# Scores of two attention heads in one group of products, in turn on the upper and the lower 64 rows of the array

## The chip, the cores and the metric

The kernel runs on one core of a Trainium2 chip. The metric is the device time of one execution in microseconds (us). Each kernel is run several times on the same chip, and a profiled execution leaves the trace from which the rows below are taken. The engines are named as in the profile: PE is the matrix unit TensorE and PEld its weight loads, DVE the vector engine, ACT the scalar engine, POOL GpSimd, and SP the engine whose queue issues the DMA transfers.

## The reference

The program is two blocks of two layers each, on 256 rows of width 1024. The change lies in the second block. Each of its layers projects the normed rows by `w_in`, runs three attentions over the 256 positions, merges them by `w_out`, and adds a cross-attention to a memory of 256 rows. Two of the three attentions matter here, each with six heads of dimension 64:

```
def moba_attention(q, k, v):              # 6 heads; 256 positions are a single block of 256,
    ...                                   # so each query sees only its own block, causally
    s_own = jnp.einsum('bhqd,bhld->bhql', qi, ko).astype(jnp.float32) * scale
    s_own = jnp.where(to[None, :] <= tq[:, None], s_own, -jnp.inf)
    p = jax.nn.softmax(jnp.concatenate([s_sel, s_own], axis=-1), axis=-1)
    ...
def stick_breaking_attention(q, k, v):    # 6 heads, strictly causal
    ...
    z = jnp.einsum('bhqd,bhkd->bhqk', qi, k).astype(jnp.float32) * scale
    mask = kpos[None, :] < (q0 + jnp.arange(Q_BLOCK))[:, None]
    log_beta = jax.nn.log_sigmoid(z)
    log_1m_beta = jnp.where(mask, log_beta - z, 0.0)
    between = lax.cumsum(log_1m_beta, axis=3, reverse=True) - log_1m_beta
    w = jnp.where(mask, jnp.exp(log_beta + between), 0.0)
    ...
```

The third, `diff`, has eight score heads of dimension 32 and is not changed.

## The kernel before

Every product of fp32 data is made of three products of rounded halves: a value is stored as a high part and a low part (`HH` and `HL` for the normed rows, `wh` and `wl` for weights), and high×high, high×low and low×high are added up in PSUM. `linear` and `linear_T` do this for the projections, with all 128 rows of the array, in products of 512, 384 or 256 columns into the PSUM tiles `lin`. Their weights are split into halves on ACT, DVE and POOL as they arrive.

The queries and keys of `moba` and of `stick` lie transposed in the tiles `QA` and `KX` of shape [128, 2, 3, 256]: head h is on partitions 0 to 63 if h is even and on 64 to 127 if it is odd, the second index is the high or the low part, the third the pair of heads. A score product therefore contracts over 64 partitions and uses the upper or the lower 64 rows of the array. `head_terms` lists a head's three (query, key) terms. Each head needs six products: for `moba` three of 128 columns (queries 0 to 127 against keys 0 to 127) and three of 256 (queries 128 to 255 against all keys), followed in `causal_scores` by a product that adds the mask (`identb` as weights, `trib` streamed); for `stick` three of 256 columns and three of 128, with the keys as weights. That is 24 heads in the two layers and 144 such products. They are written to a PSUM bank of the ring `aux`, which has four banks and is shared with transposes and other small products.

What follows a `moba` head is `causal_P`: for each of its two query tiles a maximum on DVE (`tensor_reduce`), and an exponential on ACT that also adds up its row; then a reciprocal, a scaling, three transposes on PE, and the product with the values for two heads at once (`pair_out`). After a `stick` head come absolute value, exponential and logarithm on ACT, differences on DVE, a mask on POOL, a product with a triangle of ones (`sums`), an exponential, and `pair_out`. `pipeline` writes the stages of six heads in a staggered order.

The order in which instructions stand in each engine's queue is not that in which the code is written. Every call goes to an object of the class `Plan`, which records an operation with its predecessors and an assumed cost (`cost`), and at the end `order` lays all of them out with a list scheduler (`run_list`) and issues them. Some operations may go to one of two engines (`either`), and that too is decided there. An operation is one call, so the scheduler is free to put other products between two products of one head; only what is written under `joined()` becomes one operation, whose instructions stay together. All instructions have the line of the call in `issue` (L459 before), so rows are told apart by their tiles.

Of the kernel before, what the change touches and what calls it, by code (L numbers as in the profile page):

```python
# [182 lines left out]
class Plan:  # L183
# [24 lines left out]
        self.later = {}  # L208

    @contextmanager  # L210
    def joined(self):


        self.joint = []
        yield
        self.joint = None

    def where(self, v):
# [247 lines left out]
class Net:  # L466
# [1219 lines left out]
    def causal_P(self, ps, first=None):  # L1686
# [9 lines left out]
        nc.vector.reciprocal(ri, rs)  # L1696
        return P, ri

    def causal_scores(self, terms):

        nc = self.nc
        ps = self.aux_ps()
        for qt in range(2):
            o = ps[:, 0:128] if qt == 0 else ps[:, 128:384]
            for a, (q, k) in enumerate(terms):
                nc.tensor.matmul(o, q[:, qt * 128:qt * 128 + 128], k[:, :128 * (qt + 1)],
                                 start=qt == 0 and a == 0, stop=False, skip_group_check=True)
        nc.tensor.matmul(ps.rearrange("p (a b) -> p a b", a=2)[:, :, 0:128], self.identb,
                         self.trib.unsqueeze(1).to_broadcast([128, 2, 128]), start=False, stop=True, skip_group_check=True)
        return ps  # L1710

    def causal_T(self, P):
# [48 lines left out]
    def moba(self, z, v, g, mh, ml):  # L1761
        nc = self.nc
        q = self.t([128, 2, 3, 256], F32R, "QA")
        k = self.t([128, 2, 3, 256], F32R, "KX")
        for t in range(2):
            self.partial_rope(z[:, t].rearrange("p (h d) -> p h d", h=12), self.cs16, t, 12, 16)
            for a, dst, scale in ((0, q, 0.125), (1, k, 1.0)):
                ps = self.aux_ps()
                for c in range(3):
                    nc.tensor.transpose(ps[:, c * 128:c * 128 + 128], z[:, t, (3 * a + c) * 128:(3 * a + c + 1) * 128], self.ident)  # L1770
                s = slice(t * 128, t * 128 + 128)
                self.split_evac(dst[:, 0, :, s], dst[:, 1, :, s], ps[:, :384].rearrange("p (c q) -> p c q", c=3), scale)
        self.silu_T(g)
        st = {}

        def scores(h):
            P, ri = self.causal_P(self.causal_scores(self.head_terms(q, k, h)))
            for qt, sl in ((0, slice(0, 128)), (1, slice(128, 384))):
                self.scaled(P[:, sl], P[:, sl], ri[:, qt:qt + 1])
            st[h] = P  # L1780

        def transposes(h):
            st[h] = self.causal_T(st[h])

        def values(h):
            if h % 2:
                self.pair_out(h // 2, [st.pop(h - 1), st.pop(h)], v, g[:, h // 2], mh[:, h // 2], ml[:, h // 2])
        self.pipeline(((scores, 0), (transposes, 2), (values, 3)), 6, 1300)
# [87 lines left out]
    def stick(self, q, k, v, g, mh, ml):  # L1876
        nc = self.nc
        self.silu_T(g)
        diag = (slice(0, 128), slice(256, 384))
        st = {}  # L1880

        def scores(h):
            ps = self.aux_ps()
            terms = self.head_terms(q, k, h)
            for o, ks, qs in ((ps[:, 0:256], slice(0, 128), slice(0, 256)), (ps[:, 256:384], slice(128, 256), slice(128, 256))):
                for a, (qq, kk) in enumerate(terms):
                    nc.tensor.matmul(o, kk[:, ks], qq[:, qs], start=a == 0, stop=a == 2, skip_group_check=True)
            zz = ps[:, 0:384]
            e = self.t([128, 384], F32, "S2")
            nc.scalar.activation(e, zz, AF.Abs)  # L1890
            nc.scalar.activation(e, e, AF.Exp, scale=-1.0)
            nc.scalar.activation(e, e, AF.Ln, bias=1.0, scale=1.0)
            lb = self.t([128, 384], F32, "PT")
            nc.vector.scalar_tensor_tensor(out=lb, in0=zz, scalar=0.0, in1=e, op0=ALU.min, op1=ALU.subtract)
            nc.vector.tensor_tensor(out=e, in0=lb, in1=zz, op=ALU.subtract)
            for d in diag:
                nc.gpsimd.tensor_tensor(out=e[:, d], in0=e[:, d], in1=self.strict, op=ALU.mult)
            st[h] = lb, e

        def sums(h):  # L1900
            lb, e = st[h]
            pb = self.aux_ps()
            nc.tensor.matmul(pb[:, 0:256], self.suf, e[:, 0:256], start=True, stop=False, skip_group_check=True)
            nc.tensor.matmul(pb[:, 128:256], self.ones, e[:, 256:384], start=False, stop=True, skip_group_check=True)
            nc.tensor.matmul(pb[:, 256:384], self.suf, e[:, 256:384], start=True, stop=True, skip_group_check=True)
            nc.vector.tensor_tensor(out=lb, in0=pb[:, 0:384], in1=lb, op=ALU.add)
            nc.scalar.activation(lb, lb, AF.Exp)
            for d in diag:
                nc.gpsimd.tensor_tensor(out=lb[:, d], in0=lb[:, d], in1=self.strict, op=ALU.mult)

        def values(h):
            if h % 2:
                self.pair_out(h // 2, [st.pop(h - 1)[0], st.pop(h)[0]], v, g[:, h // 2], mh[:, 5 + h // 2], ml[:, 5 + h // 2])
        self.pipeline(((values, 2), (sums, 1), (scores, 0)), 6, 2600)

    def keep_clock(self, n, a, b):
# [130 lines left out]
```

## Time and profile before

| | before |
|---|---|
| median of 3 runs | 2108.07 us (2106.64 to 2111.05) |
| the profiled execution's own time | 2108.64 us |
| its span in the trace | 2106.9 us |
| PE busy | 1871.4 us (89%) |
| DVE, ACT, POOL busy | 894.2, 851.7, 299.0 us |
| mean granted clock of PE | 0.936 |

The span runs from the first to the last instruction of the trace; the time of the execution is 1.7 us longer. A busy share is an average over stages with different limits. The second block begins at about 1703 us; in each of its layers `stick` comes first, then `diff`, then `moba`.

### The profile page before, as it was taken

The page shows a single profiled execution, that of the slowest core. Times are in us where ns is not written, and L with a number is a line of the kernel's source. Part 1 is how long each engine was busy: PE and PEld are TensorE (multiplying, and loading weights), DVE is VectorE, ACT ScalarE, POOL GpSimd, SP SyncE. Part 2 cuts the span into 40 slices and gives each one's busy share as a digit, 9 for nine tenths or more (in the row PEclk, how much of TensorE's full clock was granted, in tenths as well). Part 3 has the DMA queues.
Part 4 walks back from the last instruction along what each step waited for, and adds up shares of the span by engine and source line. Part 5 has one row for each costly group of instructions (what it writes and reads, how often), then busy time and mean ns, then how long its engine had stood idle before and what let it go on. Part 6 is the DMA issues. An engine that isn't in the chain of part 4 may idle for free.

```text
span 2106.9 us, 29479 instructions
## 1 busy us (share of the span) xinstructions
PE 1871.4 (89%) x11564; PEld 1155.5 (55%) x11564; DVE 894.2 (42%) x1871; ACT 851.7 (40%) x1874; POOL 299.0 (14%) x383
## 2 busy tenths in 40 slices
PE   7999999999999898879999996757666799999998
PEld 4666767774443232226666762323222287889787
DVE  3855786681020201007855720101010176766766
ACT  3664666562222122016754531101010166676666
POOL 1302330230000000004401300000000023222321
PEclk9999999999999999999999997777767699999999
DMA  9667563678999999996667799999999963345332
GB/s 336 233 227 270 183 240 123 220 269 326 400 401 421 422 421 421 422 413 222 221 220 261 280 354 419 421 421 421 420 421 421 378 189 91 116 140 170 91 121 70
DMA packets 150347, 611.72 MB, mean 290 GB/s; under 512 B 10144, under 2 KB 32320, under 8 KB 96192
## 3 DMA queue, kind: packets, MB, share of 16 engines
q1 hardware_dynamic: 150208, 609.84, 75.7%
q8 instruction: 91, 1.49, 0.3%
q14 instruction: 48, 0.39, 0.1%
HBM read 606.63 MB, written 3.16 MB: 289 GB/s over the span
## 4 chain that ended last, share of the span: by engine, by line
PE 61%; DMA 26%; DVE 6%; POOL 3%; ACT 2%; issue 2%; SPq 0%; POOLq 0%; DVEq 0%; ACTq 0%
PE lin L459 45%; PE aux L459 14%; DMA W<-w_up_e 5%; DMA W<-w_gate_e 3%; PE acc L459 2%; DMA M<-w_up_e 2%; DMA Z<-w_gate_e 2%; DMA Z<-w_down_e 2%; DMA G<-w_up_e 2%; DMA G<-w_gate_e 2%; DVE S L459 1%; POOL sm L459 1%; DVE wl L459 1%; ACT S L459 1%; DMA DFT<-w_down_e 1%
## 5 line engine op out<-in xcount | busy, mean ns | idle before, releaser
L459 DVE TENSOR_TENSOR wl<-W,wh 128x512 fp32r<-128x512 f32 (+1 forms) x509 | 355.4, 702 | 184.2 <-ACT wh L459 180.8
L459 ACT ACTIVATE wh<-W 128x512 fp32r<-128x512 f32 (+1 forms) x449 | 271.9, 608 | 284.9 <-PE lin L459 216.2
L459 DVE TENSOR_TENSOR S<-lin,S 128x512 f32<-128x512 f32 (+1 forms) x32 | 17.8, 558 | 601.1 <-PE lin L459 601.1
L459 POOL TENSOR_TENSOR wl<-W,wh 128x512 fp32r<-128x512 f32 (+1 forms) x67 | 87.9, 1315 | 923.6 <-DMA W<-w_in 419.5
L459 ACT ACTIVATE S<-lin 32x512 f32<-32x512 f32 (+2 forms) x94 | 52.1, 555 | 398.7 <-PE lin L459 397.9
L459 PE MATMUL lin<-wl,HH 128*128 128x512 f32 (+1 forms) x600 | 208.3, 400 | 3.7 <-DVE wl L459 3.0
L459 PE MATMUL lin<-wh,HL 128*128 128x512 f32 (+1 forms) x600 | 204.9, 394 | 2.8 <-DVE HL L459 1.7
L459 PE MATMUL lin<-wh,HH 128*128 128x512 f32 (+1 forms) x600 | 206.1, 398 | 0.0
L459 PE MATMUL lin<-W,S 128*32 128x256 f32 (+1 forms) x960 | 109.5, 520 | 44.1 <-DMA W<-w_gate_e 14.9
L459 PE MATMUL aux<-cst,S 128*128 128x128 f32 x620 | 124.2, 290 | 27.4 <-DVE S L459 20.2
L459 PEld LDWEIGHTS aux<-cst,S 128*128 128x128 f32 x620 | 82.2, 153 | 88.7 <-DVE S L459 41.2
L459 PEld LDWEIGHTS lin<-wl,HH 128*128 128x128 f32 x600 | 107.7, 190 | 34.4 <-DVE wl L459 9.5
L459 PEld LDWEIGHTS lin<-wh,HL 128*128 128x128 f32 x600 | 108.8, 189 | 26.4 <-issue 6.7
L459 PEld LDWEIGHTS lin<-wh,HH 128*128 128x128 f32 x600 | 108.4, 189 | 26.6 <-issue 5.6
L459 ACT ACTIVATE S<-aux 128x512 f32<-128x512 f32 (+4 forms) x134 | 64.9, 489 | 125.0 <-PE aux L459 124.2
L459 PE MATMUL lin<-wh,OL 128*128 128x512 f32 x272 | 95.3, 402 | 1.5 <-DVE OL L459 1.5
L459 PEld LDWEIGHTS lin<-W,S 128*32 128x32 f32 (+1 forms) x960 | 36.7, 135 | 104.4 <-issue 32.9
L459 ACT ACTIVATE S<-aux,sm 128x256 f32<-128x256 f32 (+2 forms) x136 | 71.4, 527 | 31.6 <-DVE sm L459 29.1
L459 PE MATMUL lin<-Z,S 128*32 128x256 f32 (+1 forms) x528 | 67.2, 522 | 17.4 <-DMA Z<-w_up_e 9.0
L459 POOL TENSOR_SCALAR sm<-sm 128x1 f32<-128x1 f32 (+3 forms) x42 | 17.2, 409 | 439.3 <-ACT G L459 383.5
L459 DVE TENSOR_REDUCE sm<-aux 128x1 f32<-128x512 f32 (+3 forms) x136 | 66.1, 500 | 26.8 <-PE aux L459 25.6
L459 PE MATMUL lin<-wh,OH 128*128 128x512 f32 x208 | 75.8, 404 | 1.5 <-ACT wh L459 1.1
(412 smaller groups left out, 3393.1 us busy)
## 6 DMA issues: line engine op xcount, KB each, us to landing
W<-w_up_e SPq DMA_DIRECT2D x65, 1024.0 KB, 18.8
W<-w_in SPq DMA_DIRECT2D x62, 1024.0 KB, 5.4
W<-w_ada SPq DMA_DIRECT2D x40, 1024.0 KB, 5.0
G<-w_gate_e SPq DMA_DIRECT2D x36, 1024.0 KB, 17.4
W<-w_down_e SPq DMA_DIRECT2D x33, 1024.0 KB, 18.5
Z<-w_gate_e SPq DMA_DIRECT2D x24, 1024.0 KB, 18.0
W<-w_in SPq DMA_DIRECT2D x32, 768.0 KB, 4.7
DFT<-w_gate_e SPq DMA_DIRECT2D x23, 1024.0 KB, 19.8
```

The lines of the kernel that those rows point to most:

```text
L459: fn(*(self.real(a) for a in args), **{k: self.real(a) for k, a in kw.items()})
```

## The change

`pair_scores` forms the scores of two heads (2c and 2c+1) as one joined operation of twelve products. Its loops run over the two column ranges, within these over the three terms, and innermost over the two heads, so that successive products use the upper and the lower 64 rows in turn, and write two different banks of `aux`. The scheduler is told a cost for the whole (`joined(cost)`): 3 × (128+256) × 0.45 = 518 ns. The mask product is cut out of `causal_scores` into `causal_mask`, which `moba` calls for both heads after the pair's products. In `stick` the flag that starts a bank afresh stands only on a bank's first product, where before each of the two column ranges had its own. Nothing else differs, and `diff` calls `causal_scores` as before.

```diff
-    def joined(self):
+    def joined(self, cost=None):
         self.joint = []
         yield
+        if cost is not None:
+            self.alts[self.joint[0]] = {0: cost}
         self.joint = None
...
+    def causal_mask(self, ps):
+        self.nc.tensor.matmul(ps.rearrange("p (a b) -> p a b", a=2)[:, :, 0:128], self.identb,
+                              self.trib.unsqueeze(1).to_broadcast([128, 2, 128]), start=False, stop=True, skip_group_check=True)
+
+    def pair_scores(self, pair, out):
+        pss = [self.aux_ps() for _ in pair]
+        n = len(pair[0])
+        with self.nc.joined(sum(3 * (m.stop - m.start) * 0.45 for _, m, _ in out)):
+            for i, (o, m, st) in enumerate(out):
+                for a in range(n):
+                    for ps, terms in zip(pss, pair):
+                        mov, sta = terms[a]
+                        self.nc.tensor.matmul(ps[:, o], sta[:, st], mov[:, m], start=i == 0 and a == 0, stop=a == n - 1, skip_group_check=True)
+        return pss
+
     def causal_scores(self, terms):
...
-        nc.tensor.matmul(ps.rearrange("p (a b) -> p a b", a=2)[:, :, 0:128], self.identb,
-                         self.trib.unsqueeze(1).to_broadcast([128, 2, 128]), start=False, stop=True, skip_group_check=True)
+        self.causal_mask(ps)
         return ps
...
         def scores(h):
-            P, ri = self.causal_P(self.causal_scores(self.head_terms(q, k, h)))
+            if h % 2 == 0:
+                pair = [[(kk, qq) for qq, kk in self.head_terms(q, k, h + j)] for j in range(2)]
+                out = ((slice(0, 128), slice(0, 128), slice(0, 128)), (slice(128, 384), slice(0, 256), slice(128, 256)))
+                st["ps"] = self.pair_scores(pair, out)
+                for ps in st["ps"]:
+                    self.causal_mask(ps)
+            P, ri = self.causal_P(st["ps"][h % 2])
...
         def scores(h):
-            ps = self.aux_ps()
-            terms = self.head_terms(q, k, h)
-            for o, ks, qs in ((ps[:, 0:256], slice(0, 128), slice(0, 256)), (ps[:, 256:384], slice(128, 256), slice(128, 256))):
-                for a, (qq, kk) in enumerate(terms):
-                    nc.tensor.matmul(o, kk[:, ks], qq[:, qs], start=a == 0, stop=a == 2, skip_group_check=True)
-            zz = ps[:, 0:384]
+            if h % 2 == 0:
+                out = ((slice(0, 256), slice(0, 256), slice(0, 128)), (slice(256, 384), slice(128, 256), slice(128, 256)))
+                st["ps"] = self.pair_scores([self.head_terms(q, k, h + j) for j in range(2)], out)
+            zz = st["ps"][h % 2][:, 0:384]
```

The scheduler lays the second block out anew. On PE, DVE, ACT and POOL the order up to the second block is the same in both kernels, and the order of DMA transfers on SP is the same throughout. Three places on PE show what moves.

The first is PE near the start of the first `stick`, where before the first products of two heads stand: `aux_1` is the bank of one head, `aux_3` that of another, `lin` products of 384 columns around them.

```order
L459 MATMUL lin_0_217<-wh_2_205,HL_18_9773 128x384
L459 MATMUL lin_0_217<-wh_0_200,HH_19_9760 128x384
L459 MATMUL aux_1_340<-QA_6_9925,KX_7_10011 128x256
L459 MATMUL aux_3_122<-QA_6_9925,KX_7_10011 128x256
L459 MATMUL lin_2_277<-wl_0_212,HH_19_9760 128x384
L459 MATMUL lin_0_217<-wl_0_212,HH_19_9760 128x384
```

After the change the same `lin` products stand there without them.

```order
L461 MATMUL lin_0_217<-wh_2_205,HL_18_9773 128x384
L461 MATMUL lin_0_217<-wh_0_200,HH_19_9760 128x384
L461 MATMUL lin_2_277<-wl_0_212,HH_19_9760 128x384
L461 MATMUL lin_0_217<-wl_0_212,HH_19_9760 128x384
L461 MATMUL lin_2_277<-wh_0_200,HL_18_9773 128x384
```

The second place is a little later on PE, where the rest of the first head's scores stand before, each product alone or nearly so between `lin` products.

```order
L459 MATMUL lin_2_277<-HH_19_9760,wh_2_205 128x256
L459 MATMUL aux_1_340<-QA_6_9925,KX_7_10011 128x256
L459 MATMUL lin_2_277<-HH_19_9760,wl_2_215 128x256
L459 MATMUL aux_1_340<-QA_6_9925,KX_7_10011 128x128
L459 MATMUL lin_2_277<-HL_18_9773,wh_2_205 128x256
L459 MATMUL aux_1_340<-QA_6_9925,KX_7_10011 128x128
L459 MATMUL lin_0_217<-wh_0_200,HH_19_9760 128x512
L459 MATMUL aux_1_340<-QA_6_9925,KX_7_10011 128x128
L459 MATMUL lin_0_217<-wl_0_212,HH_19_9760 128x512
L459 MATMUL lin_0_217<-wh_0_200,HL_18_9773 128x512
```

After the change the whole group of the first two heads stands here, in the banks `aux_1` and `aux_2` in turn; six of its twelve products follow with 128 columns.

```order
L461 MATMUL lin_2_277<-HL_18_9773,wh_2_205 128x256
L461 MATMUL lin_0_217<-wh_0_200,HH_19_9760 128x512
L461 MATMUL aux_1_340<-QA_6_9925,KX_7_10016 128x256
L461 MATMUL aux_2_119<-QA_6_9925,KX_7_10016 128x256
L461 MATMUL aux_1_340<-QA_6_9925,KX_7_10016 128x256
L461 MATMUL aux_2_119<-QA_6_9925,KX_7_10016 128x256
L461 MATMUL aux_1_340<-QA_6_9925,KX_7_10016 128x256
L461 MATMUL aux_2_119<-QA_6_9925,KX_7_10016 128x256
```

What stood strewn over some 140 rows of PE (two heads) is one piece. The third place is PE in the first `moba`. Before, a head's products alternate with `lin` products of 256 columns (`acc` is a product of another attention).

```order
L459 MATMUL lin_1_220<-HH_19_9760,wh_2_205 128x256
L459 MATMUL aux_1_340<-KX_8_10868,QA_7_10882 128x128
L459 MATMUL lin_1_220<-HH_19_9760,wl_2_215 128x256
L459 MATMUL aux_1_340<-KX_8_10868,QA_7_10882 128x128
L459 MATMUL lin_1_220<-HL_18_9773,wh_2_205 128x256
L459 MATMUL aux_1_340<-KX_8_10868,QA_7_10882 128x256
L459 MATMUL lin_1_220<-HH_19_9760,wh_2_205 128x256
L459 MATMUL aux_1_340<-KX_8_10868,QA_7_10882 128x256
L459 MATMUL lin_2_277<-HH_19_9760,wh_2_205 128x256
```

After the change the heads stand in groups of twelve. Between the mask products of the second pair, in the banks `aux_3` and `aux_0`, and the group of the third pair, which has the same two banks, these rows are found (ahead of them come the second mask and four more `lin` products of 256 columns):

```order
L461 MATMUL lin_2_277<-HH_19_9760,wl_2_215 128x256
L461 MATMUL lin_2_277<-HL_18_9773,wh_2_205 128x256
L461 MATMUL lin_0_217<-wh_0_200,XC_3_10397 128x512
L461 MATMUL lin_1_220<-wh_0_200,XC_3_10397 128x512
L461 MATMUL lin_0_217<-wl_0_212,XC_3_10397 128x512
L461 MATMUL lin_1_220<-wl_0_212,XC_3_10397 128x512
L461 MATMUL lin_0_217<-wh_0_200,KC_18_10401 128x512
L461 MATMUL lin_1_220<-wh_0_200,KC_18_10401 128x512
L461 MATMUL aux_1_340<-cst,S_3_224 128x128 x3
L461 MATMUL aux_3_122<-KX_8_10916,QA_7_10906 128x128
L461 MATMUL aux_0_177<-KX_8_10916,QA_7_10906 128x128
```

Third and second pair are parted by six `lin` products of 256 columns, six of 512 and three transposes.

## Rows read from the trace of the kernel before

**Rows 1.** The page, busy time, share of the span and instructions of each engine.
```profile
PE 1871.4 (89%) x11564; PEld 1155.5 (55%) x11564; DVE 894.2 (42%) x1871; ACT 851.7 (40%) x1874; POOL 299.0 (14%) x383
```

**Rows 2.** Windows: stretch, us, busy PE, PEld, DVE, ACT, POOL; clock, DMA share, GB/s.
```profile
1733.00:1777.00 44.00, 44.00 (x207) 31.87 (x206) 28.51 (x57) 24.89 (x51) 16.00 (x27) 1.00 0.31 90
1777.00:1806.00 29.00, 28.17 (x184) 25.60 (x182) 25.32 (x72) 23.08 (x65) 12.75 (x19) 1.00 0.45 135
1806.00:1842.00 36.00, 35.95 (x224) 28.27 (x224) 23.00 (x61) 21.10 (x62) 3.60 (x6) 0.95 0.30 104
```

**Rows 3.** Waits in 1733 to 1842: waited for, us in total, times, longest.
```profile
ACT wh L459 <- PE lin L459: 18.3, 20, 3.4
...
PE aux L459 <- DVE S L459: 0.9, 1, 0.9
```

**Rows 4.** Windows of the tile QA alone: busy PE, PEld, DVE, ACT; clock, DMA, GB/s.
```profile
1703.00:1777.00 74.00, 9.63 (x36) 5.62 (x36) 1.09 (x3) 1.08 (x3) 1.00 0.45 135
...
1908.00:1981.00 73.00, 9.75 (x36) 5.73 (x36) 0.27 (x1) 0.00 (x0) 0.98 0.45 135
...
sum 218.00, PE 34.61 PEld 21.18 DVE 3.55 ACT 3.07; mean PE 8.65 PEld 5.29 DVE 0.89 ACT 0.77
```

**Rows 5.** Timeline of PE in `stick`: start, us, what; x2 is two in succession.
```profile
1733.67 0.61 PE L459 MATMUL lin<-wh,HH 128*128 128x512 f32 x2
1734.12 0.61 PE L459 MATMUL lin<-wl,HH 128*128 128x512 f32 x2
1734.67 0.50 PE L459 MATMUL aux<-QA,KX 64*128 64x256 f32 x2
...
1735.76 0.43 PE L459 MATMUL aux<-QA,KX 64*128 64x128 f32 x2
...
1736.79 0.33 PE L459 MATMUL aux<-QA,KX 64*128 64x128 f32 x1
...
1737.62 0.63 PE L459 MATMUL lin<-wh,HL 128*128 128x512 f32 x2
```

**Rows 6.** Timeline of PE in `moba`, single products, and two `lin` products in succession.
```profile
1815.56 0.32 PE L459 MATMUL aux<-KX,QA 64*128 64x128 f32 x1
...
1816.13 0.38 PE L459 MATMUL aux<-KX,QA 64*128 64x256 f32 x1
...
2029.34 0.28 PE L459 MATMUL lin<-HH,wl 128*128 128x256 f32 x1
2029.46 0.28 PE L459 MATMUL lin<-HL,wh 128*128 128x256 f32 x1
```

**Rows 7.** Timeline of PE in `moba`, strings of nine and of six on one half.
```profile
1822.56 1.29 PE L459 MATMUL aux<-KX,QA 64*128 64x128 f32 x9
...
1827.75 0.63 PE L459 MATMUL lin<-wl,XC 128*128 128x512 f32 x2
1828.31 0.95 PE L459 MATMUL aux<-KX,QA 64*128 64x128 f32 x6
1829.20 0.28 PE L459 MATMUL aux<-trib,identb 128*128 128x256 bf16 x1
```

**Rows 8.** Timelines of PE and PEld, products of two heads on different halves.
```profile
1712.57 0.39 PE L459 MATMUL aux<-QA,KX 64*128 64x256 f32 x2
...
1712.57 0.19 PEld L459 LDWEIGHTS aux<-QA,KX 64*128 64x128 f32 x2 [0.26 <-issue]
...
2028.55 0.62 PE L459 MATMUL aux<-KX,QA 64*128 64x256 f32 x5
```

**Rows 9.** Windows, columns as in rows 2, a stretch of lower clock.
```profile
1818.00:1821.00 3.00, 3.00 (x14) 2.91 (x15) 1.53 (x4) 0.87 (x3) 2.14 (x3) 0.50 0.01 3
```

**Rows 10.** Timelines of ACT and DVE behind one head of `moba`.
```profile
1833.34 0.37 ACT L459 ACTIVATE S<-aux,sm 128x128 f32<-128x128 f32 x1
...
1834.05 0.20 ACT L459 ACTIVATION_READ_ACCUMULATOR S<-aux,sm 128x1 f32 x1
...
1833.01 0.62 DVE L459 TENSOR_REDUCE sm<-aux 128x1 f32<-128x128 f32 x2 [0.56 <-PE aux L459]
```

## The prediction, made before the changed kernel was run

> **What bounds the kernel now.** I read the page first: TensorE (PE) is busy 89% of 2106.9 us and no other engine half of it [rows 1]. Since the change touches only the scores of `stick` and `moba`, I then cut the second block into stretches [rows 2]. Around the scores of the first layer (1733 to 1777 `stick`, 1806 to 1842 `moba`; the second layer repeats the picture from 1934 and 2011) PE is busy in all but 0.05 us, while DVE, ACT and POOL have 35% and more to spare. The list of waits says who is late: ACT waits 18.3 us for PE's `lin` products in 1733 to 1842, and PE waits but 0.9 us for DVE there [rows 3]. So a microsecond taken from PE in these stretches is a microsecond of the kernel, until another chain becomes the later one.
>
> How much of PE are these scores? The 144 products are busy for 34.61 us in all [rows 4]. "Busy" doesn't tell what one costs its neighbours, so I looked at PE in order of time. A `linear` product of 512 columns takes 0.225 us (two between 1733.67 and 1734.12) [rows 5]. From 1734.12 to 1737.62 stand eight of them, 1.80 of 3.50 us. The other 1.70 us went on two doubles of score products and a single, whose own busy time is 0.50+0.43+0.33 = 1.26: factor 1.35. The rest lies in the neighbours: 1734.12+0.45 is 1734.57, but the double starts at 1734.67, so 0.1 goes by before a 64-row product starts, and as much again in the `lin` products after it. In `moba` a 128-column product between `lin` products of 256 columns brings the pitch to 0.57 (1815.56 to 1816.13, one `lin` in between), where two such `lin` products follow each other in 0.12: cost 0.45 for 0.32 busy, factor 1.4 [rows 6]. But six products in a string cost hardly more than their busy time: from the end of two `lin` products (1827.75+0.45 = 1828.20) to the mask product at 1829.20 it is 1.00 us for 0.95 busy, factor 1.05 [rows 7]. **What is dear is the change of height, 64 rows to 128 and back, not the product**: a single of 128 columns costs 0.45, in the string of six one product costs 0.17.
>
> By that, the cost now: `stick` has 9.63+9.75 = 19.38 us busy, in 24 singles and 24 doubles, × 1.35 = 26.2. `moba` has 34.61 − 19.38 = 15.23, of which 19 singles of some 0.34 (6.5 us) × 1.4 = 9.1, and strings of three to nine for 8.7 × 1.05 = 9.1. In all **44.4 us** for 77 excursions, 0.58 each.
>
> **What it becomes.** The 144 products stand in 12 unbroken groups of twelve, alternating between the row halves. What does a group cost? The trace of before has no twelve, but has the pieces. One head's six cost 1.00 [rows 7]. Nine on one half are busy 1.29, so a further product on the same half adds (1.29−0.95)/3 = 0.11: twelve one after another would be 1.00+6×0.11 = 1.67. Two heads on different halves do run side by side: at 1712.57 two 256-column products, of two heads by the order of the program, take 0.39 and their two weight loads 0.19 [rows 8], against 0.50 at 1734.67 where both are one head's [rows 5]; and at 2028.55 five, three of 256 columns of one half and two of 128 of the other, take 0.62. The second head therefore comes nearly free, and a group costs 1.00 if so, 1.67 if not at all. I take 1.00, the end to which both rows of different halves lie nearest, and 0.06 on average for the slower `lin` product behind it (about 0.11, in `stick` only, since `moba` has its mask product next): 12 × 1.06 = 12.7. **Removed from PE: 44.4 − 12.7 = 31.7 us** (23.6 at the other end).
>
> **The clock.** Three times in these stages the granted clock is 0.50, so 1.2 GHz in place of 2.4, in stretches of at least 3.0 us: at 1818 [rows 9], and likewise at 1934 and 2022.5. The ones at 1818 and 2022.5 follow the strings of singles in `moba`, and that at 1934 the first singles of the second `stick`. At 1818 fourteen products of 256 columns take 3.00 us, 0.21 each instead of 0.12, so 3.0 us of such a stretch lose 1.3: 3.9 in all. With PE's gaps gone I expect most of it back and take 3; none of it and 4 are the bounds.
>
> **What the change adds.** The mask product is only called from elsewhere, and no transfer moves: the queue of SP reads the same. In `stick` the first product into the second column range no longer opens with a start of its own, which costs nothing on PE. What is new are waits. Both heads' scores are ready at once, and the softmax of one occupies ACT for 0.91 us in two exponentials (1833.34 to 1834.25), with DVE's two reductions ahead of them (0.62 for two of 128 columns, so 0.3 each, and more for 256) [rows 10]. In `moba` the last pair's group writes the same two banks as the pair before it, and between them PE has only six `lin` of 256 columns, six of 512 and three transposes: 6×0.12+6×0.225+0.3 = 2.4 us, while two heads' exponentials take 1.82 on ACT behind a reduction of 0.3 and two hand-overs. If other work stands ahead on ACT, the group at PE's head waits, and all `lin` products behind it, which ACT and DVE then wait for. I allow 1 us there in each layer, and 2 more in each for the other pairs, since DVE, with 9.1−3.2 = 5.9 us less of PE and one or two of slow clock, would be busy 23.0 of some 29 us in the stretch that now is 1806 to 1842. That makes 6; the bounds are 0 (every chain keeps its slack) and 12.
>
> **Sum**, against the profiled execution's own 2108.64 us (0.6 above the median of the three runs, within their spread): 2108.6 − 31.7 − 3 + 6 = **2080 us**.
>
> **Rivals.**
> *The halves don't overlap (0.10).* The loads of the twelve weights might queue behind each other, as in the string on one half, where each further product takes 0.11 [rows 7], and a group would cost 1.67. Then 44.4 − 12×1.73 = 23.6 is removed and the time is 2088. Against it are the two loads that together take 0.19. The Trainium skill, "TensorE: Matmul & The Clock Gate", Part 2, Step-by-step, says that PE has two independent read ports to SBUF, one for the streamed operand and one for weight loads; taken strictly, twelve loads share one port, which is this rival, and 2088. The row of two loads at once says that halves share it without queueing, for two.
>
> *The time comes back as waits on DVE and ACT (0.17).* PE's 34.7 us (31.7 and the clock's 3) are lent by stages in which DVE has 13 of 36 us to spare, and ACT 15; but their work comes in chains (reduction, exponential, scaling, transposition), and both heads' chains now begin together. With half eaten it is 2108.6 − 17.3 = 2091 (0.12), with all of it 2105 to 2109 (0.05). For it: PE's own wait in `diff`, where 1777 to 1806 has DVE at 25.32 of 29 [rows 2] and PE already 0.8 idle. Against: in the stretches that change, PE almost never waits. The Trainium skill, "TensorEngine Tiling (Array Packing)", PSUM Bottleneck, warns of just this: packing the array speeds up TensorE, but not the evacuation of PSUM, which may become the bottleneck. By it, the time would be this rival's; the busy shares of the rows leave room for it only in part.
>
> *Slower (0.04).* If PE, which takes its work in a fixed order, stood after each group until both heads' chains have freed their two banks, it would lose per pair what the chain is long. The point from which it decides is 34.7/12 = 2.9 us per pair. Two heads' exponentials with their reductions, 2 × 0.91 and 2 × 0.7 at most, are 3.2 if nothing lay between; with scaling and the wait behind other work 5 us, so 12 × 5 − 34.7 = +25: 2134. Against: four banks are in the ring, so only every second pair can meet its own banks, and `lin` products stand between the groups.
>
> **How the numbers follow.** The forecast's case (waits of 0 to 12, clock 0 to 4, groups of 1.0 to 1.2) has 0.69, and runs from 2073 to 2089; its middle is 2080. The halves in series give 2088 (0.10), waits for half of it 2091 (0.12, some 2086 to 2098), waits for all of it 2107 (0.05), slower 2134 (0.04). The range from 2070 to 2094 leaves out the last two and part of the half-eaten case, some 0.14, and its lower end allows groups that cost less than one head's six do now. About 0.2%, 4.2 us, is what a measurement of this kernel tells from no change. By these cases: faster 0.91, the same 0.05, slower 0.04.
>
> **What would show it.** In the profile after, PE before 1703 us as it was; twelve groups of twelve score products, the partners starting within hundredths of a microsecond of each other and the group about 0.9 to 1.0 us long (1.5 and more: the first rival); score products busy some 12 us together instead of 34.61; stretches with `lin` products at their own pitch of 0.225 or 0.12 between the groups; the clock at 1.00 in `moba`. Waits of PE for ACT or DVE in these stretches should sum to 6 us, first of all ahead of the third pair of `moba`; 15 or more there is the second rival. The forecast is wrong if the groups are as short as I say and the span still shrinks by less than 14 us, or if a group breaks into 64-row products one after another.

## The result, and the profile after

The changed kernel takes 2074.86 us (median of 4 runs, 2072.63 to 2077.55) where the kernel before took 2108.81 beside it: ratio 0.9844, 95% interval 0.9832 to 0.9856, so 30 to 35 us less. The profiled execution took 2074.04 us, its span is 2072.3. The forecast was 2080 in a range from 2070 to 2094.

The line of busy times on the page of the changed kernel, which answers to [rows 1]: PE has lost 37 us, and is as large a share of the span as before. Its weight loads (PEld) have lost 18, and the work of no other engine changed by more than 6 us.

```profile
PE 1834.5 (89%) x11564; PEld 1137.8 (55%) x11564; DVE 891.8 (43%) x1862; ACT 850.4 (41%) x1878; POOL 305.0 (15%) x388
```

The windows of the changed kernel's stretches with `stick` and `moba` (columns as in [rows 2]). They hold less time than those of before, 34 and 26 us where it was 44 and 36, partly because other work of the second block now stands in other stretches. PE is still busy nearly throughout, with a DVE share of 83% and 75%. The clock in `moba` is 1.00, in [rows 2] it was 0.95.

```profile
1726.00:1760.00 34.00, 34.00 (x191) 27.83 (x191) 28.24 (x55) 24.45 (x51) 15.01 (x20) 1.00 0.42 124
1798.00:1824.00 26.00, 25.05 (x190) 19.73 (x188) 19.43 (x54) 19.78 (x61) 4.71 (x7) 1.00 0.31 110
```

The score products alone (windows of the tile QA, as in [rows 4]): the same 144, busy 11.18 us instead of 34.61.

```profile
1701.00:1760.00 59.00, 2.72 (x36) 2.29 (x36) 1.09 (x3) 1.08 (x3) 1.00 0.52 154
1798.00:1825.00 27.00, 2.87 (x36) 2.25 (x36) 1.11 (x2) 0.98 (x2) 1.00 0.30 106
...
sum 174.00, PE 11.18 PEld 9.09 DVE 4.48 ACT 4.16; mean PE 2.80 PEld 2.27 DVE 1.12 ACT 1.04
```

PE in order of time, first at the first group of `stick` (answers to [rows 5]), then at the first of `moba` ([rows 6, 7]). Twelve products take 0.84 us from their start to the next `lin` product and 0.89 to the mask products, as long as one head's six took before the mask (1828.31 to 1829.20 in [rows 7]). The first `lin` product behind a group takes 0.34 to the next, and then they follow at 0.23 each.

```profile
1726.41 0.39 PE L461 MATMUL lin<-wh,HH 128*128 128x512 f32 x1
1726.73 0.91 PE L461 MATMUL aux<-QA,KX 64*128 64x256 f32 x12
1727.57 0.50 PE L461 MATMUL lin<-wl,HH 128*128 128x512 f32 x1
1727.91 0.39 PE L461 MATMUL lin<-wh,HL 128*128 128x512 f32 x1
1728.14 0.39 PE L461 MATMUL lin<-wh,HH 128*128 128x512 f32 x1
1728.37 0.40 PE L461 MATMUL lin<-wl,HH 128*128 128x512 f32 x1
...
1805.13 0.96 PE L461 MATMUL aux<-KX,QA 64*128 64x128 f32 x12
1806.02 0.39 PE L461 MATMUL aux<-trib,identb 128*128 128x256 bf16 x2
```

The weight loads of the same place show where a change of height takes its time:

```profile
1727.57 0.19 PEld L461 LDWEIGHTS lin<-wl,HH 128*128 128x128 f32 x1
...
1728.14 0.19 PEld L461 LDWEIGHTS lin<-wl,HH 128*128 128x128 f32 x1
```

In a string of `lin` products a load starts together with the product before its own: the one at 1728.14 is for the product at 1728.37. The load of the first product behind the group starts only with that product, at 1727.57, and that of the group's first product likewise at 1726.73.

**Where the time went.** I matched the PE products of both traces in order and compared their start times. At the start of the second block (1710.1 before) the changed kernel is 1.6 us ahead, which no edit explains: until there both have the same order, and a second profile of the changed kernel was 2.4 ahead there. After the first layer's attentions it is 18.2 us ahead, after the second's 36.2. So the second block gives 34.7 us (34.6 in the second profile). Which product the count starts from moves this and the gains of the table below by up to 0.2. At 2045.75, behind the attentions, it loses 1.6 again to a stretch with a granted clock of 0.50 (1.2 GHz instead of 2.4), which the second profile lacks:

```profile
2045.75:2049.16 3.41, 3.41 (x12) 2.94 (x13) 1.36 (x4) 1.58 (x6) 0.00 (x0) 0.50 0.00 0
```

To add up what the scores cost PE, I took for each excursion (a run of score products with none of another kind between them) the time from the product before it to the product behind it, and on to the next, less what these `lin` products take by themselves in a string. Before that is 43.9 us, now 12.3. With the three stretches of lower clock gone, each 3.4 us long and worth some 1.5, the sum is 31.6 + 4.5 = 36.1 of gain, against 34.7 found. Of the 1.4 that are missing, 0.8 lie with the products with the values (`acc`, in `pair_out`): counted in the same way, they cost 14.9 us in 20 excursions before and 15.7 in 22 after, since the new layout parts two more of them. The waits below have 0.2, and 0.4 can't be placed.

The waits of PE in the second block, of the kernel before (columns as in [rows 3]), sum to 3.9 us:

```profile
PE aux L459 <- DVE S L459: 2.5, 3, 0.9
PE aux L459 <- ACT S L459: 0.7, 1, 0.7
PE lin L459 <- DVE HL L459: 0.5, 1, 0.5
PE lin L459 <- POOL wl L459: 0.2, 1, 0.2
```

Those of the changed kernel sum to 4.1. New waits took the place of old ones, but hardly any came on top.

```profile
PE lin L461 <- DVE wl L461: 1.9, 2, 0.9
PE aux L461 <- DVE S L461: 0.8, 1, 0.8
PE aux L461 <- ACT S L461: 0.7, 1, 0.7
PE lin L461 <- DVE HL L461: 0.5, 1, 0.5
PE lin L461 <- POOL wl L461: 0.2, 1, 0.2
```

### The profile page after: what moved, and what is told of

The parts are those of the page before. It is cut to its first block, busy times and chain, and to the rows that moved or that the text cites. A ratio compares the mean times of both kernels' runs of the same rounds, so it can differ in the third digit from the quotient of the medians.

```text
span 2072.3 us, 29481 instructions
## 1 busy us (share of the span) xinstructions
PE 1834.5 (89%) x11564; PEld 1137.8 (55%) x11564; DVE 891.8 (43%) x1862; ACT 850.4 (41%) x1878; POOL 305.0 (15%) x388
## 4 chain that ended last, share of the span: by engine, by line
PE 60%; DMA 27%; DVE 6%; POOL 3%; issue 2%; ACT 2%; SPq 0%; POOLq 0%; DVEq 0%; ACTq 0%
PE lin L461 44%; PE aux L461 13%; DMA W<-w_up_e 5%; DMA G<-w_gate_e 3%; DMA W<-w_gate_e 3%; PE acc L461 2%; DMA M<-w_up_e 2%; DMA Z<-w_gate_e 2%; DMA G<-w_up_e 2%; DMA Z<-w_down_e 2%; DVE S L461 1%; POOL sm L461 1%; DVE wl L461 1%; ACT S L461 1%; DMA OL<-w_down_e 1%
## 5 line engine op out<-in xcount | busy, mean ns | idle before, releaser
L461 ACT ACTIVATE wh<-W 128x512 fp32r<-128x512 f32 (+1 forms) x457 | 276.6, 608 | 254.3 <-PE lin L461 191.9
L461 POOL TENSOR_TENSOR wl<-W,wh 128x512 fp32r<-128x512 f32 (+1 forms) x72 | 92.5, 1287 | 920.7 <-DVE XC L461 420.2
L461 ACT ACTIVATE XC<-lin 32x256 f32<-32x256 f32 x60 | 22.5, 374 | 142.7 <-PE lin L461 142.1
L461 PE MATMUL lin<-Z,S 128*32 128x256 f32 (+1 forms) x528 | 66.4, 508 | 14.9 <-DMA Z<-w_up_e 7.7
```

Source lines behind the costliest of these rows:

```text
L461: fn(*(self.real(a) for a in args), **{k: self.real(a) for k, a in kw.items()})
```

## The experiments

**Theory A**, the prediction's: a change of height (64 rows to 128 and back) is dear, twelve groups in place of 77 excursions save most of it, and the halves running side by side save the rest. **Theory B**: the gain is one of order, since the scheduler lays out the rest better with the scores in one piece. **Theory C**: it is the alternation that counts. The first block differs by up to 4 us between profiles, so beside each median stands what the second block gains in the trace (1710.1 to 2056 us of the kernel before), with the cost of the scores worked out as above.

| kernel | median, us | its kernel before | scores on PE, us | second block gains, us |
|---|---|---|---|---|
| changed | 2074.86 | 2108.81 | 12.3 | 34.7 |
| e1, head after head | 2076.07 | 2108.37 | 16.0 | 30.0 |
| e2, alternating, not joined | 2090.54 | 2108.37 | 30.9 | 15.1 |
| e3, all on the same rows | 2081.64 | 2108.37 | 20.6 | 26.7 |
| e4, each head joined | 2087.15 | 2108.37 | 24.4 | 22.3 |
| e5, `stick` alone | 2087.31 | 2108.65 | 23.8 | 22.7 |
| e6, `moba` alone | 2092.85 | 2108.65 | 29.2 | 16.0 |
| e7, values joined too | 2071.60 | 2108.65 | 12.8 | 37.5 |
| e8, told 1000 ns | 2077.15 | 2108.65 | 13.9 | 30.8 |
| e9, before at full height | 2079.22 | 2104.77 | 16.7 | 29.0 |
| e10, two pairs in a group | 2075.45 | 2104.77 | 11.5 | 31.7 |

In e1, e2, e6, e8 and e9 the gain holds a loss of some 1.7 us to a stretch of lower clock near 1865 us, between the two layers' attentions, which the changed kernel had at 2045, beyond the stretch compared. The score products of e9 have 128 rows and are counted in the same way; 14.8 had been worked out from their widths.

**e9_before_full_height: the kernel before, its score products over all 128 rows.**

```diff
-        r, c = slice(64 * (h % 2), 64 * (h % 2) + 64), h // 2
+        r, c = slice(0, 128), h // 2
```

> The kernel before, with the same instructions in the same order on every engine, but each score product of stick and moba contracts over all 128 partitions (so it adds up two heads' scores and isn't the reference's). Nothing is grouped and nothing runs side by side; only the change of height is gone. Theory A (what is dear is the change of height): the 144 products cost what linear products of their width cost in a string, 72 x 0.12 + 72 x 0.085 = 14.8 us instead of 43.9, and the lower clock behind them may go too: 2108.6 - 29 - 3 = 2077 us, 2075 to 2081. Rival (a lone product costs 0.45 to 0.6 whatever its height, by its bank, its semaphore or its place between other shapes): within 5 us of the time before, 2103 or more.

Ratio 0.9872 (0.9856 to 0.9889), 2079.22 us. The timeline of PE shows the same eight `lin` products and the same three excursions as [rows 5]:

```profile
1731.74 0.62 PE L459 MATMUL lin<-wl,HH 128*128 128x512 f32 x2
1732.20 0.40 PE L459 MATMUL aux<-QA,KX 128*128 128x256 f32 x2
1732.43 0.63 PE L459 MATMUL lin<-wh,HL 128*128 128x512 f32 x2
1732.90 0.33 PE L459 MATMUL aux<-QA,KX 128*128 128x128 f32 x2
1733.07 0.68 PE L459 MATMUL lin<-wh,HH 128*128 128x512 f32 x2
1733.59 0.22 PE L459 MATMUL aux<-QA,KX 128*128 128x128 f32 x1
1733.65 0.68 PE L459 MATMUL lin<-wl,HH 128*128 128x512 f32 x2
1734.17 0.39 PE L459 MATMUL lin<-wh,HL 128*128 128x512 f32 x1
```

From 1731.74 to 1734.17 it is 2.43 us where it was 3.50. With 1.80 for the `lin` products, the three excursions cost 0.63 instead of 1.70. Nothing else was touched, and the order of instructions is the same, so the height alone is worth 29.0 of the 34.7 us. The weight loads bear it out: in the trace of the kernel before, the load of the first score product starts within 0.002 us of the product itself in all 77 excursions, in this one 0.02 to 0.24 us ahead of it in all 77. This rules out B as the main cause: the old layout with cheap products is nearly as fast as the new one. The kernel itself can't use all 128 rows, since each product would then add up two heads; what grouping can do is to pay for the change of height less often.

**e1_head_after_head: joined, but without alternation.**

```diff
-            for i, (o, m, st) in enumerate(out):
-                for a in range(n):
-                    for ps, terms in zip(pss, pair):
+            for ps, terms in zip(pss, pair):
+                for i, (o, m, st) in enumerate(out):
+                    for a in range(n):
```

> The two heads of a pair stay one joined group of twelve products, but the second head's six follow the first head's six instead of alternating with them. Theory A (the time came from fewer changes of height, and a smaller part from the two halves running side by side): a group takes 1.7 to 1.8 us instead of 0.84 to 0.89, so 12 x 0.85 = 10 us more than the changed kernel, 2083 to 2086 us. Theory B (most of the gain is that the scheduler, with the scores in one piece, laid out the rest better, and the length of the groups is covered by others): within 3 us of the changed kernel, 2073 to 2078. Theory C (nearly all of it comes from the alternation): most of the 34 us are lost, above 2095.

2076.07 us, within 3 us of the changed kernel as B had it, and C is ruled out. A's forecast failed here: it took the second head's products to wait for the first head's, and they don't. The group takes 1.16 to 1.18 us, not 1.7 to 1.8, while the cost of the scores (16.0) still tells what the second block gains. The group on the timeline of PE:

```profile
1725.34 1.25 PE L461 MATMUL aux<-QA,KX 64*128 64x256 f32 x12
```

And PE's instructions of that kernel grouped by shape (count, busy us, mean ns, idle before), from 1725.30 to 1725.75 only:

```profile
L461 PE MATMUL aux<-QA,KX 64*128 64x256 f32 x4 | 0.7, 332 | 0.0
```

In the program a head's three products of 256 columns come first, then three of 128, then the other head's three of 256. In the trace a fourth product of 256 columns starts before any of 128: the other head's first product (0.349 us after the group's start) starts ahead of the fourth product of the first head (0.466). Products of the free half are thus started ahead of earlier ones that wait for their own half, so much of the overlap comes without alternation in the program. Alternation is worth (1.17−0.86) × 12 = 3.7 us on PE, and the second block gains 34.7 − (30.0+1.7) = 3.0 less without it.

**e3_same_rows: alternation on one half.**

```diff
-                pair = [[(kk, qq) for qq, kk in self.head_terms(q, k, h + j)] for j in range(2)]
+                pair = [[(kk, qq) for qq, kk in self.head_terms(q, k, h)] for j in range(2)]
...
-                st["ps"] = self.pair_scores([self.head_terms(q, k, h + j) for j in range(2)], out)
+                st["ps"] = self.pair_scores([self.head_terms(q, k, h) for j in range(2)], out)
```

> The odd head of a pair takes the even head's queries and keys for its scores (so its scores are not the reference's): same groups, same banks in turn, same order, but all twelve products on one half of the rows. Theory A: a product waits for the one before it on its half, the group takes 1.5 to 1.7 us, 12 x 0.7 = 8 us more than the changed kernel, 2081 to 2085 us. If instead the two banks in turn are what lets products run side by side, the groups stay at 0.85 to 0.9 and the time at 2075. Theory B: 2073 to 2078 whatever the groups take.

2081.64 us, as A had it. The group on the timeline of PE is 1.53 us to the next `lin` product (1727.91 to 1729.44):

```profile
1727.91 1.60 PE L461 MATMUL aux<-QA,KX 64*128 64x256 f32 x12
1729.44 0.50 PE L461 MATMUL lin<-wl,HH 128*128 128x512 f32 x1
```

Twelve products take 0.84 us on two halves and 1.53 on one, with the banks in turn in both. So it is the rows, not the banks, that let them run side by side, and that is worth 34.7 − 26.7 = 8.0 us.

**e4_each_head_joined: 24 groups of six.** Each head calls `pair_scores` with itself alone.

```diff
-            if h % 2 == 0:
-                pair = [[(kk, qq) for qq, kk in self.head_terms(q, k, h + j)] for j in range(2)]
...
+            pair = [[(kk, qq) for qq, kk in self.head_terms(q, k, h)]]
...
-                st["ps"] = self.pair_scores([self.head_terms(q, k, h + j) for j in range(2)], out)
-            zz = st["ps"][h % 2][:, 0:384]
...
+            zz = self.pair_scores([self.head_terms(q, k, h)], out)[0][:, 0:384]
```

> Each head's six products are one joined group, heads aren't paired: 24 groups of six instead of 12 of twelve. Theory A: 24 x 1.0 us plus 24 x 0.06 for the product behind it = 25.4 instead of 12.3, so 13 us more than the changed kernel: 2086 to 2090 us, of which the waits may give back 1 or 2, since a head's softmax starts alone. Theory B: 2073 to 2078. Theory C: above 2095.

2087.15 us. Six products take as long as twelve on two halves (0.82 us to the next `lin` product):

```profile
1727.05 0.90 PE L461 MATMUL aux<-QA,KX 64*128 64x256 f32 x6
1727.87 0.38 PE L461 MATMUL lin<-HH,wh 128*128 128x256 f32 x1
```

The scores cost 24.4 us and the second block gains 22.3, 12.4 less than the changed kernel, as the difference of 12.1 on PE says. B expected no difference.

**e2_alternating_not_joined: alternation without the joined operation.**

```diff
-        with self.nc.joined(sum(3 * (m.stop - m.start) * 0.45 for _, m, _ in out)):
-            for i, (o, m, st) in enumerate(out):
...
+        for i, (o, m, st) in enumerate(out):
```

> The twelve products are written in alternation, but each is an operation of its own that the scheduler may place; it strews them again, over some 53 excursions instead of 12. Theory A: 53 excursions of 0.5 to 1.0 us are some 35 us instead of 12.3, so 2094 to 2100 us. Theory C (alternation is what counts, and these are written in alternation): near 2080. Theory B: near the time before, 2105 or more, since the scheduler's layout is the old kind.

2090.54 us, below A's range, above C's, and far from B's. The scheduler made 48 excursions of it, which cost 30.9 us rather than the 35 assumed. The measured gain again follows the cost on PE (43.9 − 30.9 = 13.0, and the three stretches of lower clock are gone), so A's account holds, though its forecast was too high: it reckoned with 53 excursions.

**e5_stick_alone and e6_moba_alone.** In e5 the lines of `moba` are those of before, in e6 those of `stick`.

> Only stick has the paired groups, moba is as before. By the sums of excursions in the trace of before (26.0 us for stick, 17.9 for moba) against the groups after (6.2 and 6.1), theory A gives 19.8 us for stick, and at 1934 us one stretch of lower clock worth 1.5: 2087 to 2090 us, with the two lower stretches behind moba's strings still there. If one part carries the whole gain, this is near 2075 or near 2108.

> Only moba has the paired groups, stick is as before. Theory A: 17.9 - 6.1 = 11.8 us and two stretches of lower clock worth 3.0, so 2094 us, 2092 to 2097; the two parts alone add up to the whole within 3 us. The rival, waits of moba's chains that eat its gain: 2100 or more, and more from stick.

2087.31 and 2092.85 us: gains of 21.3 and 15.8, together 37 where the whole gave 34; each has an uncertainty of some 3 or 4 us by its interval. In e6 the `stick` scores were laid out otherwise too and cost 3 us less than before, so the two aren't cleanly parts; and each alone removes two or three stretches of lower clock, where the whole removes three. One stretch of lower clock stayed in e5, where `moba` still has its strings of singles:

```profile
1809.30:1812.60 3.30, 3.30 (x17) 3.13 (x15) 1.69 (x5) 1.76 (x7) 2.20 (x3) 0.50 0.06 10
```

**e8_scheduler_cost_1000.**

```diff
-        with self.nc.joined(sum(3 * (m.stop - m.start) * 0.45 for _, m, _ in out)):
+        with self.nc.joined(1000):
```

> The changed kernel, but the scheduler is told 1000 ns for a group in place of 518, about what the trace shows (0.84 to 0.89 and the change of height). Theory A: the order differs only in places, 2072 to 2078 us. Theory B (the gain hangs on the layout that follows from the told cost): a difference of 5 us or more, either way.

2077.15 us. The told cost matters little, but it brought up the wait that the prediction feared. On the timeline of PE the third group of `moba` is 1.34 us long instead of 0.89 (1812.00 to 1813.34):

```profile
1812.00 1.41 PE L461 MATMUL aux<-KX,QA 64*128 64x128 f32 x12
1813.34 0.44 PE L461 MATMUL aux<-cst,S 128*128 128x128 f32 x2
```

Its first product starts, its second 0.456 us later; in both layers it is 0.45. The timeline of ACT shows what holds the two banks, the exponentials of the pair before, whose last parts are these:

```profile
1811.75 0.20 ACT L461 ACTIVATION_READ_ACCUMULATOR S<-aux,sm 128x1 f32 x1
...
1812.20 0.20 ACT L461 ACTIVATION_READ_ACCUMULATOR S<-aux,sm 128x1 f32 x1
```

They end at 1811.95 and 1812.40, and each time one of the two products starts 0.05 later. Two stretches of lower clock (at 1862 and 2002) make up the rest: 34.7 − 30.8 = 3.9, of which 0.9 is this wait and some 3 the two stretches.

**e10_two_pairs_in_one_group.** The told cost grows with the group.

```diff
...
-            if h % 2 == 0:
-                pair = [[(kk, qq) for qq, kk in self.head_terms(q, k, h + j)] for j in range(2)]
+            if h in (0, 4):
+                pair = [[(kk, qq) for qq, kk in self.head_terms(q, k, h + j)] for j in range(2 if h else 4)]
...
```

> The changed kernel, with heads 0 to 3 in one group of twenty-four products, on four banks, and heads 4 and 5 in one of twelve: eight groups instead of twelve. On PE alone four changes of height of some 0.2 to 0.3 us go, 1 us less: 2074. But the group holds all four banks of the ring until the softmax of the first head has read its own, and transposes and sums need banks: the rival is the prediction's, waits of PE behind the chains of ACT and DVE, 1.8 us of exponentials per pair: if they aren't covered, 4 x 1 to 3 us more, 2078 to 2086. I expect 2076 to 2080.

Ratio 0.9855 (0.9840 to 0.9869), no better than the changed kernel. The scores cost 11.5 us, 0.8 less, but the second block gains 31.7, 3.0 less. The longest of PE's waits in the second block, with those for the softmax exponentials (ACT S) and for split weights grown:

```profile
PE lin L461 <- DVE wl L461: 2.1, 3, 1.6
PE aux L461 <- ACT S L461: 1.6, 2, 0.9
PE aux L461 <- DVE S L461: 0.8, 1, 0.8
```

All its waits sum to 5.5 us, 1.4 more than in the changed kernel; where the other 2.4 went (3.0 + 0.8 − 1.4) was not settled. The two that grew most are not for banks: PE waits 1.6 us for a weight split, and 0.9 for scaled exponentials that the transposes take in (ACT has them ready at 2001.23, the transposes start at 2001.28).

**e7_values_joined: the four products of `pair_out` in one operation.**

```diff
-        for kc, q in ((0, slice(0, 256)), (1, slice(128, 256))):
-            with nc.joined():
+        with nc.joined():
+            for kc, q in ((0, slice(0, 256)), (1, slice(128, 256))):
```

> The changed kernel, and in pair_out the four products with the values, on 64 columns of the array in turn, are one joined operation instead of two: 12 returns to the full array fewer. In the trace of the changed kernel the second pair of them costs its neighbours some 0.25 to 0.4 us. Theory A (changes of shape are dear whatever the shape): 12 x 0.25 to 0.4 = 3 to 5 us less, 2070 to 2072 us. If only changes of rows cost, or if the joining makes the first product wait: 2074 to 2077.

The changed kernel, PE in order of time around the first `pair_out`:

```profile
1748.36 0.65 PE L461 MATMUL acc<-M,Z 128*64 128x256 f32 x4
1748.94 0.50 PE L461 MATMUL lin<-wl,HH 128*128 128x512 f32 x1
...
1749.61 0.44 PE L461 MATMUL acc<-M,Z 128*64 128x128 f32 x4
1749.98 0.50 PE L461 MATMUL lin<-wh,HH 128*128 128x512 f32 x1
```

And this kernel at the same point of its work:

```profile
1750.29 0.87 PE L461 MATMUL acc<-M,Z 128*64 128x256 f32 x8
1751.09 0.50 PE L461 MATMUL lin<-wh,HL 128*128 128x512 f32 x1
```

Two excursions to half the array's columns (128*64), 0.58 and 0.37 us to the next `lin` product, become one of 0.80, and the slow `lin` product behind them (0.34 to the next) comes once. In the second block 22 such excursions become 12, and what they cost falls from 15.7 to 12.3 us; the scores, laid out otherwise, cost some 0.6 more. Run again beside the changed kernel:

> The changed kernel once more, on the same chip and beside the next one, for a direct comparison: 2072 to 2078 us.

> The changed kernel with the four products with the values in one joined operation, beside the changed kernel: 2 to 4 us less than that (3.3 between medians of different calls, 2.8 in the second block of the traces), 2069 to 2074 us. If the earlier difference was the spread of the first block, no difference.

2072.55 us (2071.26 to 2075.68, ratio 0.9835) and 2070.02 (2069.62 to 2070.61, ratio 0.9820, 0.9807 to 0.9834): 2.5 us less. In the second block it is 37.5 against 34.6. This is the fastest version of the study.

## Why the prediction was right, point by point

**The bound.** Right: what left PE in these stretches left the time. The gains of e3 and e4 against the changed kernel differ from the cost of their scores on PE by 0.3 us.

**What the scores cost.** 44.4 us were worked out from factors on busy times, 43.9 is the sum over all excursions. That the change of height is the dear part was an inference from rows; e9 shows it, with 16.7.

**What the groups cost.** 12.7 forecast, 12.3 measured: 0.83 to 0.89 us a group, and no load of one half queued behind the other's. The first rival (groups of 1.67) is what e3 makes on purpose. The Trainium skill, "TensorE: Matmul & The Clock Gate", Part 2, Step-by-step, with its one read port for weights, can't be read as one load at a time: by the trace's records the loads of one half start 106 ns or more apart, but those of the two halves start in pairs, mostly 3 or 4 ns apart.

**The clock.** 3 us were taken and 4.5 came, since all three stretches were gone; one came back elsewhere in some executions, worth 1.6. What brings them on isn't settled: e8 has one in `moba` with the groups in place.

**The waits: the term that was mis-sized.** Of the 6 us that the prediction added, 0.2 came as waits in the rows. Another 0.8 went into the products with the values, whose new places the prediction had put at nothing, and 0.4 can't be placed. The place named for the waits was right and the reason wrong. Ahead of the third pair of `moba` PE does wait 0.95 us, but for a weight split on DVE. The timelines of DVE, PE and ACT there:

```profile
1808.45 0.61 DVE L461 TENSOR_REDUCE sm<-aux 128x1 f32<-128x128 f32 x2
...
1809.05 1.00 DVE L461 TENSOR_TENSOR wl<-W,wh 128x512 fp32r<-128x512 f32 x1
...
1810.11 0.74 PE L461 MATMUL lin<-wl,XC 128*128 128x512 f32 x2 [0.95 <-DVE wl L461]
...
1811.24 0.20 ACT L461 ACTIVATION_READ_ACCUMULATOR S<-aux,sm 128x1 f32 x1
...
1811.57 0.96 PE L461 MATMUL aux<-KX,QA 64*128 64x128 f32 x12
```

DVE's reductions for both heads come first, then the split (`wl`), and by the time PE has gone on to the pair's group at 1811.57 both banks are free, but only just: the last exponential that reads one ends at 1811.44. So the wait that the prediction named missed by 0.13 us here, and in e8 it came. Before, PE waited as long for DVE in this layer (0.9, [rows 3]), so a wait changed its place and not its size. The profiled execution is 5.9 us below the sum: 4.6 by waits that did not come, 1.5 by the clock, and 1.6 by the first block's lead, against 1.6 for the late stretch and 0.1 removed less from PE. The waits and the clock were both off to the slow side; that the first block's lead and the late stretch cancel is luck. One end of the forecast's case is worked out too low: with groups of 1.2, waits of 12 and no clock back it is 2091, not 2089.

**The rivals.** The time didn't come back as waits, so the rule on PSUM evacuation (the Trainium skill, "TensorEngine Tiling (Array Packing)", PSUM Bottleneck) did not bind here: DVE went to 75% of the `moba` stretch and PE still set the pace. The wait for banks shows plainly in e8, with 0.45 us in each layer. The prediction's last rival took PE to work in a fixed order, which e1 shows not to hold between the two halves.

## What to carry to other kernels

Where products of less than full height or width stand singly between full ones, count the changes of shape, not the products: here an excursion cost 0.4 to 0.6 us with one product or with two, and 1.03 with twelve on two halves. A scheduler that prices products one by one can't see that. Group them as one operation, first of all to make the changes few, and fill both halves of the array while there; alternating the halves in the program is the smaller gain. Then look for other products of the same kind, as `pair_out` was, and measure before groups grow: twenty-four products on four banks (e10) gained nothing over twelve on two, for reasons not settled.

## What was unexpected of the hardware

PE starts products out of the program's order when they use different row halves: in e1 the seventh product of a group starts 0.349 us after the group's first, the fourth at 0.466. A group of twelve in the order head after head takes 1.17 us, between the 0.83 to 0.89 of alternation and the 1.52 to 1.59 of a single half.
